# A two-layer decoder trunk with routed experts: weights laid out in load order, the last expert pair summed in PSUM, and the overflow flag read earlier

## The chip, the cores and the metric

The kernel runs on one NeuronCore of one Trainium2 chip. Its engines work side by side and meet through semaphores: TensorE (PE, with its weight loads PEld), VectorE (DVE), ScalarE (ACT), GpSimd (POOL) and SyncE (SP), which issues most of the loads. The metric is the device time of one execution in microseconds, as the median of several runs. A profile is taken of one execution.

## The reference, cut to what matters

```python
for l in range(2):                                   # 256 tokens, 1024 channels, float32
    mod = silu(c) @ w_ada[l] + b_ada[l]              # sh1, sc1, g1, sh2, sc2, g2
    h = modulate(rms_norm(x, mixer_norm_g[l]), sh1, sc1)
    proj = h @ w_in[l]                               # conv branch, pool branch, two gates
    y_a = conformer_conv_branch(...)                 # 31-tap depthwise conv, layer norm, w_conv_out
    y_b = pool_branch(...)                           # window means, pool_w
    x = x + g1 * ((gate_a * y_a + gate_b * y_b) @ w_out[l])
    h2 = modulate(rms_norm(x, ffn_norm_g[l]), sh2, sc2)
    # 4 groups of 8 experts: the best group, in it the best 2 experts of each token
    x = x + g2 * sum over the 2 chosen experts of weight * (silu(h2 @ w_g) * (h2 @ w_u)) @ w_d
return rms_norm(x, final_norm_g)
```

An expert has three matrices: gate and up (1024 x 256 each) and down (256 x 1024), 3 MB in float32. All 32 experts of both layers are read, since the tokens between them choose any.

## The kernel before, in words

**Load stream.** All large weights go through one list, `stream` (`plan`), in the order in which they are used: `w_ada`, `w_in`, `pool_w`, `w_conv_out`, `w_out`, then the experts in pairs. Each entry is one tile of 128 partitions x 2048 floats (1 MB). `issue` takes entries from the list as long as `room` finds a buffer: 14 in a ring, and up to five work tiles that lend their place (`SPARE`). `done(key)` marks a tile as used and calls `issue` again. The issuing engine is SP; it takes its loads strictly in order, and each waits for its buffer to be free. The program gives its loads one of eight completion semaphores in turn, so a load also waits until the one eight before it has landed. Small loads (`trickle`, and `fz` on ScalarE's queue, L1204) take their turn among the eight.

An expert pair has six tiles: for each of two experts the first four of eight k steps of gate and up together (two loads of 512 KB into one tile), then the last four, then two down tiles. `w_in` alone is laid out on the host so that a tile is one contiguous piece of 8 KB per partition; the others are read from their natural layout in pieces of 4 KB per partition, and the down tiles of the last pair in pieces of 2 KB.

**Routing.** `route` finishes the mixer's output projection, normalizes, computes the router, finds groups and experts, and gathers the tokens of all experts into one sorted row by matmuls with one-hot matrices: `gather(0)` for the first half of the channels, `flush()` (pending small work), `gather(1)` for the second. `windows` computes the start of each expert's window of 64 slots and a flag, 1 if any expert has more than 64 tokens. `overflow` reads that flag into registers of PE, ACT, DVE and POOL (L988) and branches (L989) round a long body that handles the excess tokens; with these inputs no instruction of the body is in the trace. For layer 0's branch a fixed hint "likely taken" stands at the kernel's start; layer 1's has none. The scheduler puts the first of block 0's matmuls ahead of the branch on PE.

**Experts.** `experts` runs 16 blocks, one for a pair, 64 slots for each expert (`XTW`). In block b: 16 matmuls of gate and up (L1118; each is two instructions in the profile), Silu, product with the routing weight (L1127), scatter matmuls of the pair before, which add its result to the tokens (L1073, L1074, high and low part), transposes to `aT` (L1133, copied at L1135), the adds into `xs` (L1081), and the down matmuls (L1093). A down half is scaled (L1099) and split into a rounded part and a rest (L1100, L1104) for the scatter. PE, DVE and ACT keep the order in which this is written. After the last pair the scatter, the adds, the squares (L340), the row scale (`sm`, L344, and a power on POOL) and, in layer 1, `finish` with four output loads on SP follow.

Of the kernel before, what the change touches and what calls it, by code (L numbers as in the profile page):

```python
# [18 lines left out]
P = 128  # L19
D = 1024  # L20
# [30 lines left out]
def trunk(ctx, tc, x, c, w_ada, b_ada, w_in, ada_cols, mix_rows, router, pool_w, w_conv_out, w_out,  # L51
          w_expert_gate, w_expert_up, w_expert_down, final_norm_g, out):
# [49 lines left out]
    def issue():  # L102
        while state["issued"] < len(stream):
            key, src, (a, b), q = stream[state["issued"]]
# [12 lines left out]
            trickle()  # L117
# [8 lines left out]
    def plan_ada(l, m, part=range(4)):  # L126
        v = w_ada[l].rearrange("(p k) n -> p k n", k=KC)
        for i in part:
            plan(("ada", l, m, i), v[:, 2 * i:2 * i + 2, m * D:(m + 1) * D], (2, D))

    def plan_in(l, g):
        shape = (KC, 256) if g < 2 else (4, 512)
        for i in range(2):
            yield ("in", l, g, i), w_in[l, 2 * g + i].rearrange("p (a b) -> p a b", b=shape[1]), shape

    def plan_out(l):
        for nm, w, n in (("co", w_conv_out, 2), ("wo", w_out, 4)):
            v = w[l].rearrange("(j p) n -> p j n", p=P)
            for i in range(n):
                plan((nm, l, i), v[:, 2 * i:2 * i + 2, :], (2, D))  # L140

    def plan_pair(l, e):
        ents = []
        for h in range(2):
            for j in range(2):
                ents.append((("gu", l, e + j, h),
                             tuple(w[l, e + j].rearrange("(p k) h -> p k h", k=KC)[:, 4 * h:4 * h + 4, :]
                                   for w in (w_expert_gate, w_expert_up)), (KC, DE)))
        wd = w_expert_down[l, e:e + 2].rearrange("e (j p) n -> p e j n", p=P)
        for j in range(2):  # L150
            if e + 2 < NE:
                ents.append((("ed", l, e + j), wd[:, j], (2, D)))
            else:
                ents.append((("ed", l, e + j), tuple(wd[:, z, :, 512 * j:512 * j + 512] for z in range(2)), (4, 512)))
# [1150 lines left out]
```

## Time and profile before

| | us |
|---|---|
| median of 3 runs (851.02 to 852.24) | 851.8 |
| the profiled execution's own time | 852.07 |
| its span, first to last instruction | 850.2 |

| engine | busy us | share of the span |
|---|---|---|
| PE | 778.5 | 92% |
| PEld | 454.4 | 53% |
| DVE | 505.6 | 59% |
| ACT | 277.0 | 33% |
| POOL | 198.2 | 23% |
| DMA queue of SP | | 89.6% |

A matmul that waits for its operand in the middle of a stream can count as busy, so PE's share says little; the timeline of one instruction per block says more. The load rate by stretch is the other thing to look at: 298 MB are moved, 351 GB/s in the mean, with stretches above 400 and below 200. A line is named as L1118; a group's count is written x32; what stands in brackets behind a line is the idle time before it and who ended it.

### The profile page before, as it was taken

The page shows a single profiled execution, that of the slowest core. Times are in us where ns is not written, and L with a number is a line of the kernel's source. Part 1 is how long each engine was busy: PE and PEld are TensorE (multiplying, and loading weights), DVE is VectorE, ACT ScalarE, POOL GpSimd, SP SyncE. Part 2 cuts the span into 40 slices and gives each one's busy share as a digit, 9 for nine tenths or more (in the row PEclk, how much of TensorE's full clock was granted, in tenths as well). Part 3 has the DMA queues.
Part 4 walks back from the last instruction along what each step waited for, and adds up shares of the span by engine and source line. Part 5 has one row for each costly group of instructions (what it writes and reads, how often), then busy time and mean ns, then how long its engine had stood idle before and what let it go on. Part 6 is the DMA issues. An engine that isn't in the chain of part 4 may idle for free. (4 is left out here: it accounts for less than half of the span.)

```text
span 850.2 us, 11978 instructions
## 1 busy us (share of the span) xinstructions
PE 778.5 (92%) x4382; PEld 454.4 (53%) x4382; DVE 505.6 (59%) x1023; ACT 277.0 (33%) x494; POOL 198.2 (23%) x133
## 2 busy tenths in 40 slices
PE   4599999997899999999879999999779999999985
PEld 2389986755333433343349998686523333333432
DVE  2369984976344644545376997497734554544545
ACT  2254544434122222222145454543322222222212
POOL 1258972510000000000034898161000000000001
PEclk9699999999999999999989999999889999999998
DMA  9999758969999999999999954797579998999993
GB/s 358 413 421 411 270 174 333 358 238 403 393 409 408 409 410 402 409 409 409 403 417 420 381 182 149 293 385 256 193 264 366 409 405 316 408 410 408 409 408 119
DMA packets 78080, 298.39 MB, mean 351 GB/s; under 512 B 7349, under 2 KB 7861, under 8 KB 74426
## 3 DMA queue, kind: packets, MB, share of 16 engines
q1 hardware_dynamic: 77448, 296.44, 89.6%
q10 hardware_dynamic: 434, 1.06, 0.3%
q8 instruction: 37, 0.61, 0.3%
q14 instruction: 33, 0.27, 0.1%
q0 software_dynamic: 128, 0.02, 0.0%
HBM read 296.44 MB, written 1.05 MB: 350 GB/s over the span
## 5 line engine op out<-in xcount | busy, mean ns | idle before, releaser
L1118 PE MATMUL pb<-wt,XTW 128*64 128x512 f32 x872 | 219.6, 593 | 12.9 <-DMA wt<-in_w_expert_up_dram 8.2
L414 POOL TENSOR_TENSOR wlo<-wt,whi 128x1024 fp32r<-128x1024 f32 x60 | 147.3, 2466 | 88.5 <-ACT whi L412 64.8
L1118 PEld LDWEIGHTS pb<-wt,XTW 128*64 128x64 f32 x872 | 73.6, 137 | 131.3 <-issue 124.5
L1127 DVE SCALAR_TENSOR_TENSOR sl<-sl,rtile,pb 128x256 f32<-128x256 f32 x32 | 15.4, 480 | 164.4 <-ACT sl L1126 164.4
L473 DVE SCALAR_TENSOR_TENSOR pd<-vpad,cols,pd 128x256 f32<-128x256 f32 x232 | 106.9, 488 | 5.7
L412 ACT CAST whi<-wt 128x1024 fp32r<-128x1024 f32 x80 | 82.8, 1049 | 73.8 <-PE pb L352 40.8
L1093 PE MATMUL pd<-wt,aT 128*64 128x512 f32 x360 | 102.7, 618 | 1.8 <-DVE aT L1135 0.5
L1100 ACT CAST yhl<-y 128x512 fp32r<-128x512 f32 x64 | 39.6, 619 | 137.9 <-DVE y L1099 137.9
L351 PE MATMUL pa<-hhl,whi 128*128 128x256 f32 x224 | 66.7, 298 | 5.2 <-ACT hhl L386 5.2
L1126 ACT ACTIVATE sl<-pb 128x256 f32<-128x256 f32 x32 | 12.3, 385 | 172.7 <-PE pb L1118 172.7
L352 PE MATMUL pa<-hhl,whi 128*128 128x256 f32 x224 | 65.6, 293 | 0.3
L353 PE MATMUL pa<-hhl,wlo 128*128 128x256 f32 x224 | 64.5, 288 | 0.6 <-POOL wlo L414 0.6
L351 PE MATMUL pb<-hhl,whi 128*128 128x256 f32 x224 | 63.6, 284 | 0.0
L297 PE MATMUL pd<-wt,cb 128*32 128x512 f32 x384 | 51.4, 623 | 13.1 <-DMA wt<-in_w_ada_dram 13.0
L352 PE MATMUL pb<-hhl,whi 128*128 128x256 f32 x224 | 62.7, 280 | 0.0
L353 PE MATMUL pb<-hhl,wlo 128*128 128x256 f32 x224 | 62.6, 279 | 0.0
L1093 PEld LDWEIGHTS pd<-wt,aT 128*64 128x64 f32 x360 | 29.1, 141 | 59.4 <-issue 39.2
L1104 DVE TENSOR_TENSOR yhl<-y,yhl 128x512 fp32r<-128x512 f32 x64 | 44.3, 693 | 22.0 <-ACT yhl L1100 22.0
L392 POOL MEMSET vpad<- 128x120 f32 x2 | 0.4, 200 | 242.5 <-DVE sl L1127 242.5
L1118 PE MATMUL pb<-wx,XTW 128*64 128x512 f32 x152 | 55.1, 593 | 0.0
L1093 PE MATMUL pd<-wx,aT 128*64 128x512 f32 x152 | 52.7, 610 | 0.8 <-DVE aT L1135 0.5
L1099 DVE TENSOR_TENSOR y<-pd,gb 128x512 f32<-128x512 f32 x64 | 44.0, 688 | 15.4 <-PE pd L1093 15.4
(257 smaller groups left out, 1345.5 us busy)
## 6 DMA issues: line engine op xcount, KB each, us to landing
wt<-in_w_expert_gate_dram SPq DMA_DIRECT2D x109, 512.0 KB, 11.5
wt<-in_w_expert_up_dram SPq DMA_DIRECT2D x109, 512.0 KB, 12.8
wt<-in_w_ada_dram SPq DMA_DIRECT2D x48, 1024.0 KB, 13.7
wt<-in_w_expert_down_dram SPq DMA_DIRECT2D x41, 1024.0 KB, 11.7
wt<-in_w_in_dram SPq DMA_DIRECT2D x28, 1024.0 KB, 20.1
wx<-in_w_expert_down_dram SPq DMA_DIRECT2D x19, 1024.0 KB, 12.0
wx<-in_w_expert_gate_dram SPq DMA_DIRECT2D x19, 512.0 KB, 11.1
wx<-in_w_expert_up_dram SPq DMA_DIRECT2D x19, 512.0 KB, 10.2
```

Source lines behind the costliest of these rows:

```text
L297: nc.tensor.matmul(ps[j:j + 32, :], cb[:, 2 * i + a, :], halves(w[:, a, :], h), start=i == 0, stop=i == 3)
L351: nc.tensor.matmul(o, ah, bh, start=start, stop=False, skip_group_check=True)
L352: nc.tensor.matmul(o, ah, bl, start=False, stop=False, skip_group_check=True)
L353: nc.tensor.matmul(o, al, bh, start=False, stop=stop, skip_group_check=True)
L412: nc.scalar.copy(hi, wv)
L414: eng.tensor_tensor(lo, wv, hi.bitcast(F32), op=OP.subtract)
L473: nc.vector.scalar_tensor_tensor(acc[:, j, :] if t == CONV_K - 1 else a, src, w, a, op0=OP.mult, op1=OP.add)
L1093: nc.tensor.matmul(o[64 * j:64 * j + 64, :], aTs[b][:, h, 64 * j:64 * j + 64], wv[j][:, h, :], start=h == 0, stop=h == 1)
L1099: nc.vector.tensor_tensor(y, downs.pop(n), s["g2"][:, n * 512:(n + 1) * 512], op=OP.mult)
L1100: nc.scalar.copy(ys[b][0][:, n * 512:(n + 1) * 512], y)
L1104: nc.vector.tensor_tensor(yl, downs.pop(("y", n)), yh.bitcast(F32), op=OP.subtract)
L1118: nc.tensor.matmul(p[64 * j:64 * j + 64], XT[:, k, 64 * j:64 * j + 64], w[j][:, :, kk, :], start=k == 0, stop=k == KC - 1)
```

## The change

1. All weights are brought on the host into the order of their tiles, so that each tile is one load of 8 KB per partition; gate and up become one array, and a tile of theirs one load in place of two. In the last pair the four tiles of the second half of k are regrouped: each holds two k steps for both experts, gate and up. The overflow body reads the new arrays.
2. The flag is read behind `gather(0)`, and a hint that takes the register's value is put there for both layers' branches; the fixed hint at the start goes away. Reading the register's value, a hint of 0 means the side that skips the body.
3. In layer 1 the last block first copies `xs` into four PSUM banks (`hold`), and the scatter of pairs 14 and 15 adds onto these; the second down half of pair 15 goes through without the split, as an fp32 matmul of 256 columns twice per token half. Squares and final products read PSUM (`last`), and one of the four output issues is ScalarE's.

```diff
@@ issue
-            v = t[:, :a * b].rearrange("p (a b) -> p a b", b=b)
-            if isinstance(src, tuple):
-                v = v.rearrange("p (i k) h -> p i k h", i=2)
-                for i, sr in enumerate(src):
-                    nc.sync.dma_start(out=v[:, i], in_=sr)
-            else:
-                nc.sync.dma_start(out=v, in_=src)
+            v = t[:, :src.shape[-1]]
+            nc.sync.dma_start(out=v, in_=src)
...
@@ plan_pair
+        ents = [(("gu", l, e + j, h), w_gate_up[l, e + j, h], (4, 2, DE) if h and e + 2 == NE else (2, 4, DE))
+                for h in range(2) for j in range(2)]
+        ents += [(("ed", l, e + j), w_down[l, e + j], (2, D) if e + 2 < NE else (2, 2, 512)) for j in range(2)]
@@ route
         gather(0)
+        r["flag"] = nc.values_load(r["fl"][0:1, 0:1], engines=[E.PE, E.Activation, E.DVE, E.Pool], min_val=0, max_val=1)
+        tc.mark_branch_hint_location(f"ov{l}", hint=r["flag"], engines=(E.PE, E.DVE, E.Activation))
         flush()
         gather(1)
@@ overflow
-        flag = nc.values_load(r["fl"][0:1, 0:1], engines=eng, min_val=0, max_val=1)
-        with (tc.If(flag > 0, label="ov0") if l == 0 else tc.If(flag > 0)):
+        with tc.If(r["flag"] > 0, label=f"ov{l}"):
@@ experts
+        def gate_up(b, p, XT, h):
+            w = need(*(("gu", l, 2 * b + j, h) for j in range(2)))
+            for kk in range(4):
+                k = 4 * h + kk
+                for j in range(2):
+                    wv = w[kk // 2][:, 2 * j:2 * j + 2, kk % 2, :] if h and b == nb - 1 else w[j][:, :, kk, :]
+                    nc.tensor.matmul(p[64 * j:64 * j + 64], XT[:, k, 64 * j:64 * j + 64], wv,
+                                     start=k == 0, stop=k == KC - 1)
...
+        def hold():
+            for h in range(2):
+                for tt in range(TT):
+                    t = sums[h, tt] = ((pa, pa), (pd, pb))[h][tt]([P, 512])
+                    nc.scalar.copy(t, xs[:, tt, h * 512:(h + 1) * 512])
+
+        def onto(h, tt, G, y, c=slice(0, 512)):
...
+            nc.tensor.matmul(sums[h, tt][:, c], G, y, start=False, stop=True, skip_group_check=True)
@@ blocks
+                fin = l + 1 == DEPTH and b == nb - 1
+                if fin:
+                    hold()
+                gate_up(b, p, XT, 0)
+                if fin:
+                    for h in range(2):
+                        for tt in range(TT):
+                            onto(h, tt, GTs[b - 1], ys[b - 1][0])
+                            onto(h, tt, GTs[b - 1], ys[b - 1][1])
+                gate_up(b, p, XT, 1)
...
+        def last(b):
...
+            down(b, 0)
+            os = [f([P, 256]) for f in (pd, pt)]
+            for z in range(2):
+                cs = slice(256 * z, 256 * z + 256)
+                for h in range(2):
+                    for j in range(2):
+                        nc.tensor.matmul(os[z][64 * j:64 * j + 64, :], aTs[b][:, h, 64 * j:64 * j + 64], wd[:, j, h, cs],
+                                         start=h == 0, stop=h == 1)
+            gain(b, 0)
+            yc = two.tile([P, 512], F32, name="y", tag="part", bufs=3)
+            for z in range(2):
+                cs = slice(256 * z, 256 * z + 256)
+                nc.vector.tensor_tensor(yc[:, cs], os[z], s["g2"][:, 512 + 256 * z:768 + 256 * z], op=OP.mult)
+                if z == 0:
+                    rest(b, 0)
+            for q in range(2):
+                for tt in range(TT):
+                    onto(0, tt, GTs[b], ys[b][q])
+            for z in range(2):
+                cs = slice(256 * z, 256 * z + 256)
+                for tt in range(TT):
+                    onto(1, tt, GTs[b], yc[:, cs], cs)
+            for tt in range(TT):
+                nc.scalar.activation(junk[:, h0], sums[0, tt], AF.Square, scale=sq, accum_out=ss[tt][:, 0:1])
+                nc.vector.tensor_tensor(xn[:, tt, h0], sums[0, tt], fin_g["b"][:, h0], op=OP.mult)
+            for tt in range(TT):
+                nc.scalar.activation(junk[:, h1], sums[1, tt], AF.Square, scale=sq, accum_out=ss[tt][:, 1:2])
+            rss = [rms_scale(tt, ss[tt]) for tt in range(TT)]
+            for tt in range(TT):
+                nc.scalar.activation(xn[:, tt, h0], xn[:, tt, h0], AF.Identity, scale=rss[tt])
+                nc.vector.scalar_tensor_tensor(xn[:, tt, h1], sums[1, tt], rss[tt], fin_g["b"][:, h1],
+                                               op0=OP.mult, op1=OP.mult)
+                for z, hs in enumerate((h0, h1)):
+                    (nc.scalar if tt > z else nc.sync).dma_start(out=out[0, tt * P:(tt + 1) * P, hs], in_=xn[:, tt, hs])
@@ start of the program
-    tc.mark_branch_hint_location("ov0", hint="LikelyTaken", engines=(E.PE, E.DVE, E.Activation))
```

## Rows read from the trace of the kernel before

**Rows 1.** Busy by stretch: engines, granted PE clock, DMA share, GB/s.
```profile
40.00:60.00 20.00, 19.39 (x159) 16.38 (x159) 9.98 (x14) 9.64 (x11) 13.06 (x6) 0.96 1.01 420
...
140.00:160.00 20.00, 19.55 (x135) 17.79 (x133) 14.41 (x23) 11.74 (x20) 11.45 (x11) 1.00 1.03 410
...
200.00:220.00 20.00, 18.40 (x108) 9.88 (x107) 7.95 (x37) 8.39 (x17) 0.00 (x0) 1.00 1.01 384
...
440.00:460.00 20.00, 17.74 (x122) 15.17 (x123) 11.95 (x16) 10.59 (x14) 10.80 (x6) 0.83 1.02 422
...
690.00:700.00 10.00, 9.95 (x48) 3.95 (x44) 4.55 (x9) 1.99 (x6) 0.00 (x0) 1.00 1.03 410
```

**Rows 2.** Timeline of VectorE, the copy to aT: start, duration, what.
```profile
239.95 0.42 DVE L1135 COPY aT<-pt 128x256 f32<-128x256 f32 x1 [0.28 <-PE pt L1133]
...
381.30 0.42 DVE L1135 COPY aT<-pt 128x256 f32<-128x256 f32 x1 [0.28 <-PE pt L1133]
...
427.26 0.42 DVE L1135 COPY aT<-pt 128x256 f32<-128x256 f32 x1 [0.31 <-PE pt L1133]
...
645.18 0.42 DVE L1135 COPY aT<-pt 128x256 f32<-128x256 f32 x1 [0.28 <-PE pt L1133]
...
747.98 0.42 DVE L1135 COPY aT<-pt 128x256 f32<-128x256 f32 x1 [0.28 <-PE pt L1133]
...
834.41 0.42 DVE L1135 COPY aT<-pt 128x256 f32<-128x256 f32 x1 [0.33 <-PE pt L1133]
```

**Rows 3.** Timeline of TensorE, the last matmuls of gate and up, both layers.
```profile
421.80 3.62 PE L1118 MATMUL pb<-wt,XTW 128*64 128x512 f32 x14 [1.47 <-DMA wt<-in_w_expert_up_dram]
...
828.93 3.62 PE L1118 MATMUL pb<-wt,XTW 128*64 128x512 f32 x14 [1.47 <-DMA wt<-in_w_expert_up_dram]
```

**Rows 4.** Timeline of TensorE in the first 30 us.
```profile
27.54 1.69 PE L297 MATMUL pd<-wt,cb 128*32 128x512 f32 x8 [1.48 <-DMA wt<-in_w_ada_dram]
```

**Rows 5.** Timeline around the branch, layer 0 (first row) and layer 1.
```profile
209.78 0.29 DVE L970 TENSOR_SCALAR rq<-io,rtile 128x128 f32<-128x128 f32 x1 [0.87 <-DVEq L989]
...
614.18 5.36 PE L1118 MATMUL pb<-wt,XTW 128*64 128x512 f32 x22 [1.40 <-ACT XTW L1056]
...
616.51 0.45 ACT L925 ACTIVATE rtile<-rtile 128x8 f32<-128x8 f32 x3
...
621.37 2.76 PE L1118 MATMUL pb<-wt,XTW 128*64 128x512 f32 x10 [1.83 <-PEq L989]
...
622.27 0.16 DVE L944 TENSOR_REDUCE rtile<-rtile 128x2 f32<-128x8 f32 x1 [6.55 <-DVEq L989]
...
625.00 1.07 PE L974 MATMUL pd<-rtile,rq 128*128 128x16 f32 x8 [0.88 <-DVE rtile L962]
```

**Rows 6.** Chain that ended last, a later block of layer 1: start, us, what.
```profile
649.32 6.87 PE pb L1118 x32
...
656.61 0.24 PE pa L1074
```

**Rows 7.** Timeline of TensorE between the gather halves, layer 0.
```profile
199.77 1.96 PE L320 MATMUL pd<-part,Q 128*128 128x512 f32 x4 [3.00 <-DVE part L308]
```

**Rows 8.** Waits of SP's load queue, 690 to 706: total, times, longest.
```profile
SPq L114 <- DMA fz<-in_final_norm_g_dram: 9.4, 1, 9.4
```

**Rows 9.** Timeline of ScalarE's queue, the same stretch.
```profile
701.94 0.49 ACTq L1204 DMA_DIRECT2D fz<-in_final_norm_g_dram  x1
```

**Rows 10.** Busy by stretch, layer 1, columns as in rows 1.
```profile
632.00:636.00 4.00, 4.00 (x14) 1.22 (x12) 1.96 (x4) 0.62 (x1) 0.00 (x0) 0.57 0.16 67
...
700.00:720.00 20.00, 19.95 (x94) 7.26 (x90) 9.11 (x16) 4.12 (x9) 0.00 (x0) 1.00 0.81 304
```

**Rows 11.** Timeline of single operations: an fp32 matmul group, a ScalarE write, the row scale.
```profile
625.92 1.11 PE L977 MATMUL pd<-dg,ones 128*128 128x256 f32 x4
...
837.65 0.62 ACT L1100 CAST yhl<-y 128x512 fp32r<-128x512 f32 x1 [4.68 <-DVE y L1099]
...
843.05 0.83 DVE L344 SCALAR_TENSOR_TENSOR sm<-ss,deps 128x1 f32<-128x1 f32 x2 [0.19 <-ACT xn L340]
```

More of the change, by code (lines that the diff above doesn't have):

```diff
@@ L103, in issue @@
         while state["issued"] < len(stream):
-            key, src, (a, b), q = stream[state["issued"]]
+            key, src, shape, q = stream[state["issued"]]
             t = room(key, q)
@@ L1127, in blocks @@
                 nc.vector.scalar_tensor_tensor(sl, sl, r["ws"][:, b:b + 1], p[:, 1, :], op0=OP.mult, op1=OP.mult)
-                for part in range(3):
-                    scatter(b - 1, part)
-                add(b - 1, 0)
+                if not fin:
+                    for part in range(3):
+                        scatter(b - 1, part)
+                    add(b - 1, 0)
                 q = pt([P, 2, P])
@@ L1135, in blocks @@
                 nc.vector.tensor_copy(aTs[b], q)
-                scatter(b - 1, 3)
+                if not fin:
+                    scatter(b - 1, 3)
                 window(b + 1)
-                for part in range(1, 4):
+                for part in range(1, 0 if fin else 4):
                     add(b - 1, part)
@@ L1158, in blocks @@
             b = nb - 1
+            if l + 1 == DEPTH:
+                return last(b)
             xn = work.tile([P, TT, D], F32, name="xn", tag="X0")
@@ L1183, in blocks @@
                 rss.append(rms_scale(tt, sss[tt]))
-            if l + 1 == DEPTH:
-                finish(xn, rss)
           return xn, rss
+        def last(b):
+            xn = work.tile([P, TT, D], F32, name="xn", tag="X0")
+            junk = work.tile([P, D], F32, name="junk", tag="bigA")
+            ss = [two.tile([P, 2], F32, name="ss") for _ in range(TT)]
+            h0, h1 = slice(0, 512), slice(512, 1024)
+            down(b, 0)
+            done(("ed", l, 2 * b))
+            wd, = need(("ed", l, 2 * b + 1))
+            os = [f([P, 256]) for f in (pd, pt)]
+            for z in range(2):
+                cs = slice(256 * z, 256 * z + 256)
+                for h in range(2):
+                    for j in range(2):
+                        nc.tensor.matmul(os[z][64 * j:64 * j + 64, :], aTs[b][:, h, 64 * j:64 * j + 64], wd[:, j, h, cs],
[7 more added lines that the diff above has]
+                    rest(b, 0)
+            for q in range(2):
+                for tt in range(TT):
[4 more added lines that the diff above has]
+                    onto(1, tt, GTs[b], yc[:, cs], cs)
+            sq = float(D) ** -0.5
+            for tt in range(TT):
[10 more added lines that the diff above has]
+                    (nc.scalar if tt > z else nc.sync).dma_start(out=out[0, tt * P:(tt + 1) * P, hs], in_=xn[:, tt, hs])
+            return xn, rss
@@ L1282, in laid_out @@
     r["pool_w"] = a["pool_w"].transpose(0, 2, 1, 3).reshape(DEPTH, P, 4 * 256)
+    v = a["w_ada"].reshape(DEPTH, P, 4, 2, 6, D).transpose(0, 4, 2, 1, 3, 5)
+    r["w_ada"] = v.reshape(DEPTH, 6, 4, P, 2048)
+    for k in ("w_conv_out", "w_out"):
+        r[k] = a[k].reshape(DEPTH, -1, 2, P, D).transpose(0, 1, 3, 2, 4).reshape(DEPTH, -1, P, 2048)
+    gu = np.stack([a[k].reshape(DEPTH, NE, P, 2, 4 * DE) for k in ("w_expert_gate", "w_expert_up")], 4)
+    gu = np.ascontiguousarray(gu.transpose(0, 1, 3, 2, 4, 5)).reshape(DEPTH, NE, 2, P, 2048)
+    for q in range(2):
+        ks = slice(4 + 2 * q, 6 + 2 * q)
+        v = np.stack([a[k].reshape(DEPTH, NE, P, KC, DE)[:, z, :, ks] for z in (NE - 2, NE - 1)
+                      for k in ("w_expert_gate", "w_expert_up")], 2)
+        gu[:, NE - 2 + q, 1] = v.reshape(DEPTH, P, 2048)
+    r["w_gate_up"] = gu
+    v = a["w_expert_down"].reshape(DEPTH, NE, 2, P, D).transpose(0, 1, 3, 2, 4)
+    wd = np.ascontiguousarray(v).reshape(DEPTH, NE, P, 2048)
+    for n in range(2):
+        wd[:, NE - 2 + n] = v[:, NE - 2:, :, :, 512 * n:512 * n + 512].transpose(0, 2, 1, 3, 4).reshape(DEPTH, P, 2048)
+    r["w_down"] = wd
     return r
```

77 lines of the change are left out of this document (32 added, 45 removed).

## The prediction, on record before the result

> **What bounds the kernel now.** I read the busy shares and load rates by stretch first, then VectorE's timeline of one instruction that stands once in each expert pair (`aT`), then the waits of TensorE, VectorE and the load queue, then the last 20 us line by line.
>
> The loads first. Where the already contiguous tiles of `w_in` stream (8 KB in one piece per partition), the windows give 420 and 422 GB/s; where `w_ada` or the experts stream (4 KB pieces) they give 410 [rows 1]. A tile is 1,048,576 bytes, so it costs 2.557 us at 410 and 2.491 us at 421: 0.067 us between them. One window, at the start of layer 0's experts, has only 384 [rows 1].
>
> Then the pairs. A pair is six tiles, so 15.3 us of loading. Its computing shows in the `aT` rows: in layer 0 from 239.95 to 381.30 there are eleven steps of 12.85 us, in layer 1 from 645.18 to 747.98 eight of 12.85 [rows 2]. So TensorE sets the step as long as tiles lie ready, and it falls back to the loads once it has eaten their lead. Without that fall, `aT` of pair 15 would come at 239.95 + 14 x 12.85 = 419.85 in layer 0 (it comes at 427.26) and at 645.18 + 14 x 12.85 = 825.08 in layer 1 (it comes at 834.41) [rows 2]. These 7.4 and 9.3 us are all that faster loads can return inside the experts; the mixers between are bound by computing. In both layers the last pair starts its last matmuls on the landing of an up tile [rows 3].
>
> **The change part by part.**
>
> *Contiguous tiles, front.* The first projection waits for the eighth `w_ada` tile, at 27.54 [rows 4]. 8 x 0.067 = **0.5 us**. Bounds: 0 if the rate does not move; I take the rate of `w_in`, the nearest row, which has the very layout that all get. The `w_conv_out` and `w_out` loads wait for free buffers, so their edit is worth nothing; no cover is lost, since they only get shorter.
>
> *Contiguous tiles, layer 0.* From about 220 the loads run without a hole to the end of the layer: (427.3 - 220) / 2.557 = 81 tiles, x 0.067 = 5.4 us. The last pair's four second-half tiles (both experts, gate and up) are regrouped so that the last one to land holds half of the k steps for both experts: after it about half of the 14 matmuls (3.62 us) [rows 3] are left, 1.8 us less. 427.26 - 5.4 - 1.8 = 420.06 against TensorE's own 419.85: `aT` at about 420.1, **7.2 us** gained. Next in line is TensorE itself, 0.2 us behind. The two down tiles land 2.5 and 5.0 us after the last gate/up tile and are wanted some 4 and 6 us after it.
>
> *The flag, layer 1.* VectorE stands 6.55 us at the branch before L944, and TensorE 1.83 us there in the middle of the first pair's matmuls; this branch has no hint. In layer 0, which is hinted, VectorE stands 0.87 us [rows 5]. With a hint TensorE does its 22 + 10 matmuls in one piece, 6.87 us as in the later blocks [rows 6]: 614.18 + 6.87 = 621.05. VectorE's part up to L974 takes 625.00 - 622.27 = 2.7 us and can begin after the three exponentials, which end at 616.96, so it is through before 620. L974 then starts at about 621.15 in place of 625.00 [rows 5]: **3.85 us**. Next in line is TensorE. ScalarE's own branch ends within its wait for L977's result. The register is 0 when the body is skipped, and 0 is what the hint reads as the skipping side, so it says in both layers what the fixed hint said in layer 0.
>
> *The flag read between the gather halves.* One register load on each of PE, ACT, DVE and POOL and a hint on three of them, behind gather(0), in both layers. Behind it on VectorE stand the two L308 operations, for which TensorE waits 3.00 us in layer 0 [rows 7], and behind those gather(1), the windows and the experts. The trace does not show a register load by itself. From above it costs VectorE's 0.87 us at layer 0's branch, which holds such a load and a jump [rows 5]; from below it gains as much, since the same load goes away before the branch. I take 0: it can run beside the two writes of gathered columns that VectorE still has in hand, and the branch where it goes away is not on TensorE's path. On POOL nothing waits behind it.
>
> *Fewer, larger loads.* The program hands its loads eight completion semaphores in turn, and a load waits for the one eight before it. In layer 1 the small `fz` load on ScalarE's queue takes one of them; SP stands 9.4 us for it [rows 8], since it is issued only at 701.94, behind pair 5's work [rows 9]; the stretch 700 to 720 moves 304 GB/s, 20 x (1 - 304/410) = 5.2 us of loading lost [rows 10]. The load that stands comes six tiles behind `fz` today; with one load per tile it comes eight behind, with seven tiles (17 us) in the queue before it, more than the 9.4 us. I expect the hole to go. It is worth 0 to 5.2 us by whether the loads bind there.
>
> *Layer 1, who binds.* The load stream picks up after the first pair, at about 637 (67 GB/s before) [rows 10]. From 637.5 to the last up tile at 828.9 [rows 3] are 70 tiles: 179.0 us in 191.4, so 12.4 lost, 5.2 of it the hole. Now the start is 0.5 + 7.2 + 3.85 = 11.55 earlier, 625.95; + 70 x 2.491 + 7.2 = 807.5. TensorE's path: 825.08 - 11.55 = 813.5. In the last pair the eight sum matmuls (0.24 us each [rows 6], 1.9 us) stand ahead of the second half instead of beside the activation; the transposes then come a little sooner. Bounds + 0 and + 1.9; I take + 1.5, so `aT` at **815.0**. It wants the last tile 3.3 us earlier, at 811.7, and that has been there for 4 us. So layer 1 becomes bound by TensorE from end to end: 834.41 - 815.0 = **19.4 us** with all that went before.
>
> *The last pair in PSUM.* `hold` is four ScalarE writes of 128x512 (0.62 us each, as L1100 [rows 11]) beside the first half's matmuls; each sum needs only its own. Bounds 0 to 2.5 us; I take 0. The end: from `aT` to the first `sm` are 8.6 us today, and 7.2 more to the end of the span [rows 11]. New path from `aT`: first down half 2.0 (eight matmuls of the pair's step), two half-width parts of 1.2, the sums of the first half 1.0, then four fp32 matmuls of 256 columns, 0.49 us each as two of them in L977 [rows 11], 1.95, then the Square of the second half and its sum 0.9: 8.2 to `sm` of the second token half, where today's 8.6 is the first's. The adds into `xs` and POOL's product go away, and one of the four output issues moves from SP to ScalarE. I put the end at 14.4 us after `aT`, against 15.8: **1.4 us** gained. Bounds: 1.9 gained, or 1.5 lost if TensorE runs at its half clock there, where the fp32 matmuls and the down parts double.
>
> *Sum.* 850.2 - 19.4 - 1.4 = 829.4 us span; with the 1.9 us around it (852.07 - 850.2) 831.3; the profiled run lies 0.3 above the median of 851.8, so **831.0 us**.
>
> One rule of the Trainium skill speaks for less: "DMA: Bandwidth & Descriptors", section "Why small descriptors are slow (HBM only)", gives a fixed 3 cycles per packet on top of one per 32 bytes. By it, an estimate, going from 4 KB to 8 KB saves 1.2%, 0.03 us of a tile and not the 0.067 of [rows 1], and the sum would be the first rival's.
>
> **The rivals.**
>
> *Half the gain in rate* (0.033 us a tile). For it: the two rates come from different stretches; against it: two windows of `w_in` agree within 1%, and those of 4 KB as well. Layer 0's `aT`: 427.26 - 1.8 - 2.7 = 422.8, 2.7 later than forecast, the front 0.25; layer 1 stays with TensorE: **834.0 us**. With no gain at all layer 0 comes 5.4 later, the front 0.5, and layer 1 just meets its loads, + 0.4: **837.3**.
>
> *The register hint does nothing.* Then layer 1 keeps its stand (3.85 lost from the forecast) and layer 0 gets one: TensorE's gap there would be layer 1's 2.5 us between its 22 and 10 matmuls. 831.0 + 6.35 = **837.4**. For it: no register hint is in the trace; against: in layer 0 ten microseconds lie between the place of the read (199.77) and the branch (209.78) [rows 5, 7], and the fixed hint works there.
>
> *Slower: the expert tiles come at the rate of the weak window*, 384 GB/s [rows 1], 2.731 us each, because eight whole tiles in flight slow each other. Layer 0 ends 12.3 us later than now (81 x 0.174 - 1.8); layer 1's loads start at 637.5 + 12.3 - 3.85 = 645.95, the last tile lands at 645.95 + 191.2 + 7.2 = 844.3, `aT` at 847.6: **863.6**. It decides from about 395 GB/s downward. Against it: `w_in` runs with eight whole tiles in flight already, at 421.
>
> *Faster still.* TensorE's clock stood at 0.57 after pair 0 of layer 1 [rows 10], and that pair took longer than 12.85; with fewer holes ahead of it up to 2.5 us return: **828.5**.
>
> **How the numbers follow.** Forecast 0.57, faster still 0.08, half the gain 0.12, none 0.06, hint without effect 0.12, slower 0.03, within 0.2% 0.02 (two failing together with a worse end). The range 827.5 to 838.5 holds all but the doubles and the slow case. About 0.2%, 1.7 us, is what a measurement can tell from no change: faster 0.95, same 0.02, slower 0.03.
>
> **What would show it.** Expert windows at 420 GB/s or more; `aT` of layer 0 stepping by 12.85 to the end, pair 15 near 419.6; no stand over 1 us at the branch in either layer; no hole behind pair 5; layer 1's last matmuls waiting for no load; 14.4 us from `aT` to the end. I am wrong if the experts' windows stay at 410, if a stand at the branch appears in layer 0, or if pairs still step by 15 us.

## The result, and the profile after

| | before | changed | changed, second session |
|---|---|---|---|
| median, us | 851.41 | 836.83 | 834.34 (before: 851.42) |
| ratio, 95% interval | | 0.9835, 0.9810 to 0.9859 | 0.9812, 0.9782 to 0.9841 |
| span of the profiled run, us | 850.2 | 834.6 | 833.0 |

The forecast was 831.0, range 827.5 to 838.5. The kernel is faster, by about 15 to 17 us, but 3.3 to 5.8 us of the forecast are missing. All medians here and below leave out one execution of the run `layout`, which took 1874 us. In stages, cut at VectorE's copy to `aT` (L1135 before, L1163 now), and each worked out as a difference of two such rows:

| stage, us | before | forecast | changed | second session |
|---|---|---|---|---|
| start to `aT` of layer 0, pair 0 | 225.51 | 225.0 | 226.36 | 224.72 |
| layer 0, pair 0 to pair 15 | 201.75 | 194.55 | 194.44 | 194.45 |
| layer 0 pair 15 to layer 1 pair 0 | 202.54 | 198.7 | 200.53 | 200.31 |
| layer 1, pair 0 to pair 15 | 204.61 | 196.75 | 198.90 | 199.08 |
| last `aT` to the end of the span | 15.8 | 14.4 | 14.4 | 14.4 |

The forecast's column takes its sum apart: 0.5 of the front, then 7.2 and 3.85, then layer 1's steps 15.38 + 14 x 12.85 + 1.5, rounded so that the column adds up to 829.4.

First the load rates of the changed kernel, by stretch (engines' busy time and instructions, granted PE clock, DMA share, GB/s).

```profile
140.00:160.00 20.00, 19.70 (x135) 17.94 (x134) 14.19 (x22) 11.74 (x19) 11.45 (x11) 1.00 1.02 424
...
200.00:220.00 20.00, 18.30 (x102) 9.46 (x104) 7.88 (x36) 8.34 (x17) 0.00 (x0) 0.92 0.84 326
240.00:280.00 40.00, 39.81 (x183) 15.69 (x183) 21.20 (x40) 10.38 (x25) 0.00 (x0) 1.00 1.01 421
...
700.00:720.00 20.00, 19.91 (x92) 7.56 (x92) 12.57 (x23) 5.42 (x13) 0.00 (x0) 1.00 1.02 423
```

In the last two stretches the experts stream at 421 and 423, as `w_in` did before [rows 1], and TensorE is busy for nearly all of the time. The first stretch moves `w_ada`, in one load of 1 MB per tile as before: 424, where the same stretch of [rows 1] has 410 with 4 KB pieces. The stretch 200 to 220 moves only 326, less than the 384 of [rows 1], but that is no rate: the load queue stands 11.4 us there until TensorE gives a buffer back (total, times, longest).

```profile
SPq L109 <- PE pa L829: 11.4, 1, 11.4
```

The next rows are VectorE's timeline, the copies to `aT` (start, duration, what, idle time ahead).

```profile
226.36 0.42 DVE L1163 COPY aT<-pt 128x256 f32<-128x256 f32 x1 [0.53 <-PE pt L1161]
240.90 0.42 DVE L1163 COPY aT<-pt 128x256 f32<-128x256 f32 x1 [0.28 <-PE pt L1161]
...
420.80 0.42 DVE L1163 COPY aT<-pt 128x256 f32<-128x256 f32 x1 [0.31 <-PE pt L1161]
...
636.38 0.42 DVE L1163 COPY aT<-pt 128x256 f32<-128x256 f32 x1 [0.28 <-PE pt L1161]
...
739.18 0.43 DVE L1163 COPY aT<-pt 128x256 f32<-128x256 f32 x1 [0.28 <-PE pt L1161]
...
754.10 0.42 DVE L1163 COPY aT<-pt 128x256 f32<-128x256 f32 x1 [0.28 <-PE pt L1161]
...
805.54 0.42 DVE L1163 COPY aT<-pt 128x256 f32<-128x256 f32 x1 [0.30 <-PE pt L1161]
...
820.23 0.42 DVE L1163 COPY aT<-pt 128x256 f32<-128x256 f32 x1 [0.53 <-PE pt L1161]
```

Layer 0 goes from 240.90 to 420.80 in 14 steps of 12.85: TensorE binds it from end to end, where the last three steps of [rows 2] took 45.96 us, over 15 each. In layer 1 every step from pair 1 on is 12.85 but two: 14.92 to pair 10 (739.18 to 754.10), and 14.69 to pair 15. Neither is a wait for a load. TensorE's timeline of those two places:

```profile
743.24 1.99 PE L1279 MATMUL pd<-fz,Q 128*128 128x512 f32 x4
...
809.50 3.60 PE L1108 MATMUL pb<-wt,XTW 128*64 128x512 f32 x16
813.03 1.20 PE L1130 MATMUL pa<-yhl,GT 128*128 128x512 f32 x4
...
815.10 3.65 PE L1108 MATMUL pb<-wt,XTW 128*64 128x512 f32 x16
...
819.75 0.44 PE L1161 MATMUL pt<-idc,sl 128*128 128x128 f32 x2 [1.00 <-DVE sl L1154]
```

The first is the spread of the final gain behind pair 9: two matmuls, four instructions, 1.99 us. The kernel before has the same work at the same place, TensorE's row and VectorE's next copy behind the 747.98 of [rows 2]:

```profile
752.04 1.98 PE L1208 MATMUL pd<-fz,Q 128*128 128x512 f32 x4
```

```profile
762.90 0.42 DVE L1135 COPY aT<-pt 128x256 f32<-128x256 f32 x1 [0.28 <-PE pt L1133]
```

The other rows of the changed kernel hold the eight sums of pair 14, which stand 2.07 us between the two halves of pair 15; after the second half TensorE idles 1.00 us in front of the transposes. No row of the last pair waits for a tile any more; in [rows 3] it did.

At the branch of layer 1 (L989 before, L974 now), both engines:

```profile
606.92 3.65 PE L1108 MATMUL pb<-wt,XTW 128*64 128x512 f32 x14 [1.40 <-ACT XTW L1052]
610.72 4.48 PE L1108 MATMUL pb<-wt,XTW 128*64 128x512 f32 x18
613.80 0.16 DVE L931 TENSOR_REDUCE rtile<-rtile 128x2 f32<-128x8 f32 x1 [5.34 <-DVEq L974]
616.54 1.07 PE L961 MATMUL pd<-rtile,rq 128*128 128x16 f32 x8 [1.34 <-DVE rtile L949]
```

TensorE's stand of 1.83 us [rows 5] has shrunk to 0.15 (606.92 + 3.65 to 610.72). VectorE's has only shrunk, from 6.55 to 5.34, so L961 (L974 before) still waits 1.34 us for what VectorE does behind it.

### The profile page after: what moved, and what is told of

It is laid out like the page before. It is cut to its first block, busy times and chain, and to the rows that moved or that the text cites. A ratio compares the mean times of both kernels' runs of the same rounds, so it can differ in the third digit from the quotient of the medians.

```text
span 834.6 us, 11864 instructions
## 1 busy us (share of the span) xinstructions
PE 773.9 (93%) x4394; PEld 452.6 (54%) x4394; DVE 499.2 (60%) x1017; ACT 278.0 (33%) x497; POOL 196.5 (24%) x131
## 5 line engine op out<-in xcount | busy, mean ns | idle before, releaser
L1108 PE MATMUL pb<-wt,XTW 128*64 128x512 f32 x872 | 213.8, 593 | 3.0 <-ACT XTW L1052 2.8
L1108 PEld LDWEIGHTS pb<-wt,XTW 128*64 128x64 f32 x872 | 70.0, 137 | 118.8 <-issue 112.8
L1089 PE MATMUL pd<-wt,aT 128*64 128x512 f32 x352 | 100.8, 618 | 2.2 <-DVE aT L1163 1.0
L336 PE MATMUL pa<-hhl,whi 128*128 128x256 f32 x224 | 67.6, 302 | 3.3 <-ACT hhl L371 3.3
L337 PE MATMUL pa<-hhl,whi 128*128 128x256 f32 x224 | 66.6, 297 | 1.1 <-DVE hhl L373 1.0
L331 POOL TENSOR_TENSOR rs<-sm,mhalf 128x1 f32<-128x1 f32 x10 | 7.6, 756 | 230.1 <-DVE sm L329 230.1
```

Of the source, the lines that this page charges most:

```text
L336: nc.tensor.matmul(o, ah, bh, start=start, stop=False, skip_group_check=True)
L337: nc.tensor.matmul(o, ah, bl, start=False, stop=False, skip_group_check=True)
L1089: nc.tensor.matmul(o[64 * j:64 * j + 64, :], aTs[b][:, h, 64 * j:64 * j + 64], wv[j][:, h, :], start=h == 0, stop=h == 1)
L1108: nc.tensor.matmul(p[64 * j:64 * j + 64], XT[:, k, 64 * j:64 * j + 64], wv, start=k == 0, stop=k == KC - 1)
```

## The experiments

Medians and ratios (to the kernel before, on the same chip); the stages are those of the table above, from each run's own profile.

| run | median | ratio, 95% interval | pair 0 to 15, layer 0 | between | pair 0 to 15, layer 1 | end |
|---|---|---|---|---|---|---|
| `layout` | 837.72 | 0.9833, 0.9810 to 0.9857 | 195.54 | 201.68 | 196.54 | 16.0 |
| `halves` | 843.94 | 0.9891, 0.9867 to 0.9915 | 198.16 | 200.71 | 203.51 | 14.4 |
| `tail_old` | 834.46 | 0.9802, 0.9777 to 0.9827 | 194.43 | 200.32 | 197.17 | 16.0 |
| `no_hint` | 845.30 | 0.9925, 0.9899 to 0.9951 | 193.99 | 207.46 | 198.39 | 14.4 |
| `fixed` | 839.96 | 0.9843, 0.9819 to 0.9867 | 194.43 | 204.96 | 198.41 | 14.4 |
| `sums_late` | 834.03 | 0.9785, 0.9761 to 0.9809 | 195.18 | 200.70 | 197.33 | 14.5 |
| `gain_dma` | 832.83 | 0.9776, 0.9758 to 0.9793 | 194.45 | 200.38 | 197.62 | 14.4 |
| `best1` | 836.15 | 0.9810, 0.9790 to 0.9829 | 194.42 | 204.83 | 195.25 | 14.4 |
| `after_again` | 834.34 | 0.9812, 0.9782 to 0.9841 | 194.45 | 200.31 | 199.08 | 14.4 |
| `early` | 839.21 | 0.9844, 0.9823 to 0.9866 | 195.18 | 202.79 | 198.10 | 14.4 |
| `best2` | 830.48 | 0.9750, 0.9726 to 0.9774 | 195.12 | 200.46 | 195.30 | 14.4 |
| `best3` | 832.84 | 0.9783, 0.9760 to 0.9806 | 195.19 | 202.64 | 194.25 | 14.4 |

The intervals are some 3 to 5 us wide, so edits of 1 to 2 us are read from the stages, each from one profile. Where the edits do not touch them, the stage between the layers repeats within 0.4 us; the first step of layer 0 comes at 14.5 or at 15.3 us, the first of layer 1 between 15.0 and 15.5, and the start, which is not in the table, varies from 223.4 to 226.5.

**The tiles alone (`layout`).**

```diff
-        r["flag"] = nc.values_load(r["fl"][0:1, 0:1], engines=[E.PE, E.Activation, E.DVE, E.Pool], min_val=0, max_val=1)
-        tc.mark_branch_hint_location(f"ov{l}", hint=r["flag"], engines=(E.PE, E.DVE, E.Activation))
...
+        eng = [E.PE, E.Activation, E.DVE, E.Pool]
+        flag = nc.values_load(r["fl"][0:1, 0:1], engines=eng, min_val=0, max_val=1)
+        with (tc.If(flag > 0, label="ov0") if l == 0 else tc.If(flag > 0)):
...
-            if l + 1 == DEPTH:
-                return last(b)
...
```

> The contiguous tiles (with the last pair's regrouped tiles) alone; flag, hint and the sum of the last pair as in the kernel before. Theory A (the rate carries the change: TensorE binds both layers once tiles come at 421 GB/s): aT of layer 0 steps by 12.85 us to pair 15, near 421; layer 1 keeps its stand of about 6.5 us on VectorE at the branch, its pair 15 comes near 820.7, and with the old 15.8 us end the span is 836.5 and the time about 838.5. Rival B (the flag and the PSUM sum carry a good part): aT as in A, but 841 or more. Rival C (without the early flag layer 1 starts late enough to be bound by loads again): pair steps of 15 us reappear in layer 1.

It has 837.72 against 851.79 beside it: 14.1 of the 15 to 17 us. Behind pair 0 of layer 0 its stages add up to 609.8 us, those of the kernel before to 624.7 and of the changed kernel to 608.2, so the tiles carry 14.9 of 16.5. All steps behind the first are 12.85 in both layers, but for the 14.91 to pair 10, and no load is waited for, so theory A holds. The regrouping of the last pair's tiles is part of this run and was not tried by itself. The stage between the layers gains 0.9 here without the early flag; why is open. TensorE's row at layer 1's branch is the one of before, somewhat longer:

```profile
605.79 5.37 PE L1108 MATMUL pb<-wt,XTW 128*64 128x512 f32 x22 [1.40 <-ACT XTW L1052]
613.68 2.76 PE L1108 MATMUL pb<-wt,XTW 128*64 128x512 f32 x10 [2.52 <-PEq L974]
```

**Half-size loads of the same bytes (`halves`).**

```diff
-            nc.sync.dma_start(out=v, in_=src)
+            if key[0] == "gu":
+                for z in (0, 1024):
+                    nc.sync.dma_start(out=v[:, z:z + 1024], in_=src[:, z:z + 1024])
+            else:
+                nc.sync.dma_start(out=v, in_=src)
```

> The changed kernel with each gate/up tile loaded as two loads of 512 KB with 4 KB pieces; the bytes in memory and all computing stay. Theory A (the piece's size sets the rate): expert stretches fall back to about 410 GB/s, layer 0's last pairs step by 15 us again and its pair 15 comes near 425.4 (+4.6), the stand for fz returns in layer 1, the time is about 845. Rival B (the strides of the old layout in memory set the rate, not the piece that one descriptor moves): rates stay at 420, 837. Rival C (only the number of loads in flight matters, through the eight semaphores): rates stay at 420 outside the fz stand, layer 0 steps by 12.85, and only the fz hole of layer 1 returns: 837 to 839.

Its stretches:

```profile
240.00:280.00 40.00, 39.82 (x182) 15.64 (x181) 21.19 (x40) 10.38 (x25) 0.00 (x0) 1.00 1.02 413
...
680.00:700.00 20.00, 19.95 (x94) 7.39 (x92) 10.91 (x20) 4.30 (x9) 0.00 (x0) 1.00 0.81 320
```

Four of six tiles of a pair come in 4 KB pieces here, two in 8 KB pieces: (4 x 410 + 2 x 421) / 6 = 413.7, and 413 is what stands. The order in memory is the changed kernel's, so the old strides are not the cause (rival B falls). The edit also raises the number of loads, but `w_ada`, with one load per tile in both kernels, shows the same step from 410 to 424, and layer 0's last pairs wait for loads here (1.29 us ahead of pair 14's last matmuls) without any stand for `fz` (rival C falls). So it is the size of the piece. With it the end of each layer binds on loads again: 198.16 and 203.51 us. Of the 13.0 us that the change gained in the two expert stages (201.75 + 204.61 to 194.44 + 198.90) this one edit undoes 3.7 + 4.6; 0.7 and 0.4 of these lie in the first steps, which vary by as much without an edit.

**The old end (`tail_old`).**

```diff
-                fin = l + 1 == DEPTH and b == nb - 1
+                fin = False
...
-            if l + 1 == DEPTH:
-                return last(b)
...
```

> The changed kernel with the end of the kernel before (pair 14 added by VectorE beside the activation, pair 15 added and squared as before). Theory A: pair 15's aT 1.84 us earlier (near 818.4), the end 15.8 us after it in place of 14.4, so 0.4 us less: within 0.2% of the changed kernel. Rival B (the PSUM sum is worth its 1.4 us, since the last step would be long in any case): 838.2.

The last step is 12.85 again:

```profile
802.47 0.42 DVE L1163 COPY aT<-pt 128x256 f32<-128x256 f32 x1 [0.30 <-PE pt L1161]
...
815.32 0.42 DVE L1163 COPY aT<-pt 128x256 f32<-128x256 f32 x1 [0.31 <-PE pt L1161]
```

The end takes 16.0 us in place of 14.4. So the sum in PSUM pays 1.84 ahead of `aT` and gets 1.6 back behind it. By the ratios, 0.9802 here against 0.9835 and 0.9812, no difference can be told. Theory A holds; as written, this part of the change is worth nothing that shows.

**No hint (`no_hint`)**: the line `tc.mark_branch_hint_location(...)` left out.

> The changed kernel without any hint; the flag is still read between the gather halves. Theory A (the hint does its work in layer 0 and none in layer 1): layer 0 gets a stand of about 5.3 us on VectorE, hidden behind TensorE's L282, and layer 1's stays at 5.3; TensorE loses under 1 us; time 836.5 to 838. Rival B (in layer 1 the hint saved the 1.2 us between 6.55 and 5.34): layer 1's stand goes back to 6.5 and pair 0 of layer 1 comes 1.2 us later, 838. Rival C (the hint does nothing in either layer): no stand in layer 0, the same time as the changed kernel.

Theory A is right on VectorE and wrong on TensorE; rivals B and C fall. The hint is worth far more than each said. The timelines at layer 0's branch and layer 1's:

```profile
213.03 5.34 PE L282 MATMUL pd<-wt,cb 128*32 128x512 f32 x32 [3.60 <-DVEq L973]
213.14 0.29 DVE L956 TENSOR_SCALAR rq<-io,rtile 128x128 f32<-128x128 f32 x1 [5.81 <-DVEq L973]
...
615.50 0.16 DVE L930 TENSOR_REDUCE rtile<-rtile 128x2 f32<-128x8 f32 x1 [4.92 <-DVEq L973]
615.89 1.04 PE L1107 MATMUL pb<-wt,XTW 128*64 128x512 f32 x3 [3.19 <-PEq L973]
619.22 5.91 PE L1107 MATMUL pb<-wt,XTW 128*64 128x512 f32 x15 [2.29 <-issue]
```

Without it TensorE stands 3.60 us in layer 0 and 3.19 + 2.29 in layer 1, VectorE 5.81 and 4.92. With it (changed kernel) TensorE has 0.30 and nothing, VectorE 0.24 and 5.34. So the register hint does its work on TensorE in layer 1 and on VectorE in layer 0, and none on VectorE in layer 1. TensorE's 3.60 us in layer 0 end with VectorE's sequencer (`DVEq`), so they can be VectorE's stand passed on; a stand of TensorE's own is not shown there. With the stands the start comes at 228.15, 1.7 us behind the latest without such an edit. That the stage between the layers grows by 7.0, more than TensorE's 5.5, goes with its last matmuls there running slower, 15 in 5.91 us. Behind the two stands the granted clock is at the lower of its two levels, 1.2 GHz (0.50 in the first column after the engines):

```profile
619.00:622.00 3.00, 2.78 (x8) 1.40 (x9) 0.00 (x0) 0.00 (x0) 0.00 (x0) 0.50 0.65 270
```

**A hint ahead of another branch (`fixed`).**

```diff
-        tc.mark_branch_hint_location(f"ov{l}", hint=r["flag"], engines=(E.PE, E.DVE, E.Activation))
...
+        if l + 1 < DEPTH:
+            tc.mark_branch_hint_location(f"ov{l + 1}", hint="LikelyTaken", engines=(E.PE, E.DVE, E.Activation))
...
+    tc.mark_branch_hint_location("ov0", hint="LikelyTaken", engines=(E.PE, E.DVE, E.Activation))
```

> The changed kernel, the flag read where it is, but with fixed hints: layer 0's at the program's start, layer 1's right behind layer 0's branch, some 500 VectorE instructions ahead of its own branch (the changed kernel's hint stands 19 ahead). Theory A (in layer 1 VectorE's hint comes when its next block of instructions is already being fetched, so it comes too late): the stand of 5.3 us in layer 1 goes, L961 starts 1.3 us sooner, pair 0 of layer 1 comes 1.3 to 2 us earlier. Rival B (what VectorE stands for in layer 1 is not a matter of the hint's place): the stand stays at 5 us and all times as in the changed kernel. Rival C (a hint is forgotten, or the branch between takes its place): TensorE gets the 3.2 and 2.3 us stands of the kernel without hints.

Nothing ties a fixed hint to its place, and the trace has both at the start, within the first 0.9 us, ahead of layer 0's branch. Layer 0's still works (0.2 us on VectorE). Layer 1's does not:

```profile
614.31 0.16 DVE L930 TENSOR_REDUCE rtile<-rtile 128x2 f32<-128x8 f32 x1 [5.20 <-DVEq L973]
614.72 6.17 PE L1107 MATMUL pb<-wt,XTW 128*64 128x512 f32 x18 [3.49 <-PEq L973]
```

This is rival C with one stand in place of two, 4.5 us slower between the layers. The edit did not do what it was meant to, so it says nothing on theory A. What the register does for layer 1 may then be that the hint cannot move ahead of it, and so stays behind layer 0's branch. Whether the branch between or the mere distance makes the early hint useless is not shown; a fixed hint held there by other means was not tried.

**VectorE's hint moved up (`early`).**

```diff
         def place():
+            cm = rt("cm", [P, 1])
+            nc.vector.tensor_reduce(out=cm, in_=r["rp"][:, 3, :], axis=AX.X, op=OP.max)
+            r["fl"] = rt("fl", [P, 1], I32)
+            nc.vector.tensor_scalar(r["fl"], cm, float(CAP), None, op0=OP.is_gt)
+            f0 = nc.values_load(r["fl"][0:1, 0:1], engines=[E.DVE], min_val=0, max_val=1)
+            tc.mark_branch_hint_location(f"ov{l}", hint=f0, engines=(E.DVE,))
...
-        tc.mark_branch_hint_location(f"ov{l}", hint=r["flag"], engines=(E.PE, E.DVE, E.Activation))
+        tc.mark_branch_hint_location(f"ov{l}", hint=r["flag"], engines=(E.PE, E.Activation))
```

> The changed kernel with VectorE's own register load and hint moved up: the flag is worked out first thing in the placing of the tokens, and VectorE's hint stands 42 of its instructions ahead of the branch instead of 19; TensorE's and ScalarE's stay. Theory A (VectorE's hint in layer 1 came behind the fetch of its next block, which starts 17 to 20 instructions ahead of the branch): the 5.3 us stand of layer 1 goes below 1, L961 follows TensorE's matmuls without the 1.3 us wait, pair 0 comes about 1.3 us sooner from the branch on. Rival B (the place of the hint is not what VectorE stands for): the stand stays at about 5 us. Rival C: the moved operations delay the gathers by their 0.7 us and the sum is nothing.

VectorE still stands 5.1 us, and the operations moved ahead of the one-hot matrices make the first gather wait 3.34 us for them (2.2 in the changed kernel); the gather then runs 4.11 us for 3.79, and the stage is 2.5 us longer, of which layer 1's first step gives 0.8 to 1.0 back.

```profile
595.40 4.11 PE L831 MATMUL pa<-G,xhl 128*128 128x256 f32 x16 [3.34 <-DVE G L902]
...
617.53 0.16 DVE L933 TENSOR_REDUCE rtile<-rtile 128x2 f32<-128x8 f32 x1 [5.14 <-DVEq L976]
```

This is rival B. Theory A, that the hint came too late by a few instructions, falls. What VectorE stands for is not shown. The DMA view has loads of code there (queue, count, MB, share). In the changed kernel, from 204.5 to 210.6, up to layer 0's branch, and from 608.5 to 613.8, within the stand of layer 1:

```profile
q14 instruction: 2, 0.02, 0.9%
...
q14 instruction: 2, 0.02, 1.2%
q8 instruction: 1, 0.02, 1.1%
```

In `no_hint`, from 203 to 206, ahead of layer 0's branch, and from 207.3 to 213.1, within its stand:

```profile
q14 instruction: 2, 0.02, 1.5%
...
q8 instruction: 1, 0.02, 1.1%
q14 instruction: 2, 0.02, 0.8%
```

Which engine each belongs to the profile does not say. The two ahead of layer 0's branch come with and without a hint, so they are not its work. Where VectorE stands, three more fall into the stand; where it does not, in layer 0 of the changed kernel, none comes between 209.9 and 213. That a stand is a wait for code is likely by this, but not shown, and why VectorE's hint does not help in layer 1 stays open.

**The sums behind the second half (`sums_late`).**

```diff
-                if fin:
-                    for h in range(2):
-                        for tt in range(TT):
-                            onto(h, tt, GTs[b - 1], ys[b - 1][0])
-                            onto(h, tt, GTs[b - 1], ys[b - 1][1])
                 gate_up(b, p, XT, 1)
...
+                if fin:
+                    for h, tt in ((0, 0), (0, 1), (1, 0)):
+                        onto(h, tt, GTs[b - 1], ys[b - 1][0])
+                        onto(h, tt, GTs[b - 1], ys[b - 1][1])
...
+                if fin:
+                    onto(1, 1, GTs[b - 1], ys[b - 1][0])
+                    onto(1, 1, GTs[b - 1], ys[b - 1][1])
```

> The changed kernel with the eight sum matmuls of pair 14 behind the second half of pair 15 (six beside the activation, two behind the transposes) in place of ahead of it. Theory A (TensorE binds, and the eight stood on its path with nothing beside them): pair 15's second half starts 2.0 us sooner, its down matmuls 1.5 us sooner than the changed kernel's in the distance from pair 14's aT (14.69 + 0.48 us there), so 1.5 us less in all. Rival B (the second half then waits for its tiles): no gain, a wait for the last gate/up tile ahead of L1108. Rival C (the sums behind delay pair 15's own sums by what they gain): within 0.5 us.

```profile
805.50 0.42 DVE L1162 COPY aT<-pt 128x256 f32<-128x256 f32 x1 [0.31 <-PE pt L1160]
818.35 0.42 DVE L1162 COPY aT<-pt 128x256 f32<-128x256 f32 x1 [0.91 <-PE pt L1160]
```

The step is 12.85, the end still 14.5 us: 1.84 less on the path, a little more than theory A said. With this order the sum in PSUM does gain, by the stages.

**The final gain by a load (`gain_dma`).**

```diff
-            fin_g["row"], fin_g["b"] = fz[:, 0, :], fz[:, 1, :]
-            nc.gpsimd.memset(fin_g["row"], 0.0)
-            nc.scalar.dma_start(out=fin_g["row"][0:1, :], in_=final_norm_g.rearrange("(a n) -> a n", a=1))
-        else:
...
+            fin_g["b"] = fz[:, 1, :]
+            nc.scalar.dma_start(out=fin_g["b"], in_=final_norm_g.partition_broadcast(P))
```

> The changed kernel with the final gain spread over the partitions by one load (each partition reads the same 4 KB from memory, 512 KB moved) in place of two matmuls (four instructions) and two ScalarE copies behind pair 9. Theory A: the step of 14.92 us to pair 10 of layer 1 becomes 12.85, all that follows comes 2.07 us sooner. Rival B (the larger load, or its wait among the eight semaphores, makes a hole that the tiles' lead does not cover): the step to pair 10 shrinks and a later one grows to 14 or 15 us.

```profile
736.30 0.42 DVE L1163 COPY aT<-pt 128x256 f32<-128x256 f32 x1 [0.28 <-PE pt L1161]
749.15 0.42 DVE L1163 COPY aT<-pt 128x256 f32<-128x256 f32 x1 [0.28 <-PE pt L1161]
...
800.60 0.42 DVE L1163 COPY aT<-pt 128x256 f32<-128x256 f32 x1 [0.32 <-PE pt L1161]
815.82 0.42 DVE L1163 COPY aT<-pt 128x256 f32<-128x256 f32 x1 [0.53 <-PE pt L1161]
```

The step to pair 10 is 12.85: 2.07 back. The last one grew from 14.69 to 15.22, as rival B had it in kind: 0.5 us, all of it in the first half's matmuls (4.13 us for 3.60). That they wait for a tile inside the group is likely, but the trace does not show it. The load queue stands 16.4 us for `fz` here, against 13.4 in the changed kernel.

**The three together (`best1`)**: `fixed`, `sums_late` and `gain_dma` in one.

> The three edits together: fixed early hints, the late sums, the gain by a load. Theory A: their sum, 1.5 + 2.07 + 1.3 to 2, so about 5 us below the changed kernel, near 831.8, the loads still ahead of the last pair by about 1 us. Rival B (the loads become the bound): the last pairs of layer 1 wait for tiles, and the gain is 3 us or less.

836.15: layer 1's pairs gain 3.7 us, and the fixed hint loses 4.4 between the layers, so theory A falls. Rival B comes true in part: the last two steps are 13.15 and 13.37, 0.8 us over TensorE's, with the same stand of the load queue for `fz` (16.6 us).

**The changed kernel again (`after_again`)**, unchanged, beside the next three.

> The changed kernel itself, beside the next three on one chip: 835 to 838, with the 5.3 us stand of VectorE in layer 1 and none over 0.3 us of TensorE there.

834.34, just below what was expected, with 5.0 us of VectorE's stand. Between this profile and the first the start of the program differs by 1.64 us (224.72 to 226.36) in the same instructions. Nearly all of it comes in one stretch of 4 us, where TensorE's matmuls of L305 take 3.48 us in the first profile and 1.96 in the second. The first fence is the first profile, the second this one, each with the stretch and TensorE's row.

```profile
199.00:203.00 4.00, 3.04 (x4) 1.41 (x5) 0.78 (x2) 0.58 (x1) 0.00 (x0) 0.58 1.01 414
...
199.96 3.48 PE L305 MATMUL pd<-part,Q 128*128 128x512 f32 x4 [2.96 <-DVE part L293]
```

```profile
198.00:202.00 4.00, 2.15 (x8) 1.23 (x9) 1.68 (x3) 0.74 (x2) 0.00 (x0) 1.00 1.00 410
...
199.85 1.96 PE L305 MATMUL pd<-part,Q 128*128 128x512 f32 x4 [2.98 <-DVE part L293]
```

In both, TensorE had idled some 3 us before. The granted clock is 0.58 in the one (mostly at the lower of its two levels, 1.2 GHz) and 1.00 in the other. An earlier stretch of the first profile, 186 to 190, had 0.58 as well and cost next to nothing: behind it TensorE waits for VectorE in the other profile, and the two are within 0.3 us again.

**The best version (`best2`)**: the late sums, and the gain's load in the weights' own queue (the cut shows this line against `gain_dma`).

```diff
-            nc.scalar.dma_start(out=fin_g["b"], in_=final_norm_g.partition_broadcast(P))
+            small.append((fin_g["b"], final_norm_g.partition_broadcast(P)))
```

> The changed kernel with the late sums and the final gain spread by a load, which now goes in the weights' own queue behind pair 5 in place of ScalarE's queue. Theory A (1.84 us of the sums, 2.07 us of the matmuls, and the load queue no longer stands 13 us for fz, so the last pairs do not wait for tiles): about 3.9 us below the changed kernel, near 832.5 by 836.5, and all steps of layer 1 from pair 1 on at 12.85. Rival B (the load of 512 KB costs the lead of the tiles): a step of over 13 us near the end, gain 3.4 or less.

830.48 against 834.34 beside it, ratio 0.9750 against 0.9812, and the fastest of all runs. The load queue's wait, and VectorE's copies of pairs 1 and 15 in layer 1:

```profile
SPq L109 <- DMA fz<-in_final_norm_g_dram: 0.9, 1, 0.9
```

```profile
637.45 0.43 DVE L1162 COPY aT<-pt 128x256 f32<-128x256 f32 x1 [0.27 <-PE pt L1160]
...
817.34 0.42 DVE L1162 COPY aT<-pt 128x256 f32<-128x256 f32 x1 [0.90 <-PE pt L1160]
```

(817.34 - 637.45) / 14 = 12.85: nothing but TensorE's step is left. The stage is 3.8 us shorter than the changed kernel's, the 1.84 and the 2.07 but for 0.1, as theory A had it. It ran beside `after_again`, and the two intervals do not meet.

**With the early hint as well (`best3`).**

> The kernel of the expectation before this with VectorE's early hint as well. Theory A: another 1.3 us less, near 831. Rival B (the hint's place does not matter): the same as the one before.

832.84: neither theory A nor rival B, but slower. The stage between the layers is 2.2 us longer, as in `early`, and layer 1's first step gives 1.1 back.

## Why the prediction was right, and where it was not

- **Rates: right.** Experts at about 421 GB/s, no pair of 15 us in layer 0. The two rates of [rows 1] were the two piece sizes, which `halves` and the tiles of `w_ada` show. The rule that the prediction drew from the Trainium skill, "DMA: Bandwidth & Descriptors", section "Why small descriptors are slow (HBM only)", gave an estimate of 1.2% from 4 to 8 KB; the stretches show 2.7% (410 to 421), and the measurement decides.
- **Layer 0: right**, 194.4 us against 194.55.
- **Front, 0.5 us: not to be seen.** The start scatters more than that between profiles of the same instructions (224.72 and 226.36), for the most part by the clock above. One profiled run cannot carry a term of this size there.
- **The flag in layer 1, 3.85 us: wrong in its second half.** The step that failed is VectorE's part "so it is through before 620", and with it "L974 then starts at about 621.15". TensorE's part came, and `no_hint` shows that the hint does it. VectorE's did not: 5.34 us of stand remain, and L961 waits 1.34 for it. The other failed term is "6.87 us as in the later blocks": TensorE's matmuls there take 8.28 us, from 606.92 to 615.20, at a granted clock of 1.00. The rows had it: the 22 and the 10 of [rows 5] take 5.36 + 2.76 = 8.12 us without the stand between them. From the first of them to L961 it is now 9.62 us, before 10.82, forecast 6.97. The stage gained 2.0 to 2.2, of which `layout` has 0.9 without this edit, so the flag and its hint brought some 1.2 to 1.4 of the 3.85. Of the rival "the register hint does nothing" one engine in one layer came true, which no case had priced.
- **Reading the flag early, 0: not separated.** With the hint no row speaks against it. Without a hint it costs: TensorE stands 5.5 us at layer 1's branch in `no_hint`, 2.5 in `layout`, where the read stands at the branch.
- **The hole for `fz`: half right.** The queue's stand grew from 9.4 [rows 8] to 13.4 us; the hole did not go, but the seven whole tiles ahead covered most of it: 423 GB/s in 700 to 720, where [rows 10] has 304, and 382 in the slice before, 1.9 us of loading lost for 5.2. TensorE waits for none of it.
- **Layer 1 bound by TensorE: right; its step count: wrong.** "Without that fall, `aT` of pair 15 would come at ... 645.18 + 14 x 12.85" left out that one step is longer on TensorE itself: 14.92 to pair 10, the spread of the final gain. The step stands in the trace of before too, from 747.98 [rows 2] to the next copy at 762.90; I took it for the start of the fall back to the loads, and the 1.98 us of L1208 are work and no wait. It is 2.07 us, and `gain_dma` returns it.
- **The sums ahead of the second half: right in kind**, 1.84 for 1.5. **The end: right**, 14.4 us. So this edit, forecast at about nothing in all, shows nothing (`tail_old`).

Sum of what failed, first profile: 1.35 at the start, 1.84 between the layers, 2.15 in layer 1's pairs, 0.1 gained in layer 0's: 5.2 us, which is 834.6 less the forecast span of 829.4. In the second session the start has no such error, and 3.6 are left. The first session's time lies nearest the rival without gain in rate (837.3) and that without a working hint (837.4), the second's nearest the one with half the gain (834.0). Those on the rate are refuted by the rates, that on the hint by TensorE's rows in layer 1, so a time near a rival's does not speak for it. That both times fell into the range is in part luck: it was drawn wide for other cases than the two that came, a longer step and half a working hint.

## What to carry to other kernels

Before a step of the steady state is multiplied out, look at each step that is longer and ask for the wait in it; one without a wait is work, and it stays when the loads get faster. An edit that takes work off the end is worth only what it does not put on the path ahead of it: place the new work beside an activation or a transposition in which the engine idles anyway. Where a program branches, look for the stand at the branch on each engine separately. Here a hint tied to a register computed in the same stage, and so behind the branch before, took away TensorE's stand at the second branch, and not VectorE's.

## What was not expected of the hardware

- At a branch round a body that is not run, VectorE stood 4.9 to 6.6 us and TensorE 1.8 to 5.5 us without a working hint. A hint given ahead of an earlier branch did not help TensorE at the next (3.49 us).
- The hint worked on VectorE in layer 0 (0.24 us for 5.81) and not in layer 1 (5.34, 5.14 with the hint 42 instructions ahead, 4.92 with none). Open.
- The same instructions ran with the granted clock at 0.58 in a stretch of 4 us in one execution and at 1.00 in another; the start of the program moved by 1.6 us.
